# A tuned transformer block on one core: eight operand tags in the second MLP product, and the MLP norm's weights moved from the activations to w_up

## The chip, the cores and the metric

The kernel runs on one core of a Trainium2 chip. The metric is the device time of one execution in microseconds. The kernel before takes 1678.88 us (median of 3 runs, 1674.23 to 1683.34).

## The reference, cut to what matters

The block mixes tokens with two attentions, merges them, and then runs an MLP and a gated embedding on 1024 rows of width 1024, all in float32. The change lies in the MLP:

```python
x = x + merged @ w_o
h2 = rmsnorm(x, g_mlp)            # y = x * rsqrt(mean(x*x) + eps);  h2 = y * g_mlp
u = relu(h2 @ w_up)               # 1024 x 4096
x = x + (u * u) @ w_down          # 4096 x 1024
```

`g_mlp` has one weight for each of the 1024 inner columns of the first product, that is, one for each row of `w_up`.

## The kernel before, in words

Float32 operands are split into a high part (a cast) and a low part (the residue), and each block of a product is three matmuls of 128x128 by 128x512 (`mm3`). Both MLP products are done by a 2x2 block scheme with seven products in place of eight, which needs sums of blocks on both sides.

*Before the first product.* `wo` finishes x = x + merged w_o in row blocks of 128 rows: four of the upper half (h = 0), four of the lower (h = 1). `upper_rows(s)` norms an upper block, transposes it through a DMA, adds its two halves into `R0` on GpSimd (L871), multiplies by the weights on VectorE (L872, `g_up` broadcast) and makes the operands `b11` and `b21` (`parts`: a cast on ScalarE, the residue on VectorE or GpSimd). `lower_rows(s)` is a generator: its first part norms a lower block, its second transposes it on TensorE into PSUM and forms w1 = g·v(upper k) - ra, w2 = g·v(lower k) - w1 and b22 = g·v(lower k), each as four small instructions with a per-partition weight (`scaled`, L893; L902), then t3r = w2 - ra (L907) and rb = rb - w2 (L908), on GpSimd for s < 2 and on VectorE for s = 2, 3. The operands of the activations' side are b11, b21, t1 (from w1), t2 (from w2), b22, t3 (from t3r) and t4 (from rb).

*The first product.* w_up is read in column tiles of 128 (`raw_tile` or `raw2`, 128 x 8 x 128); two of them make a pair b, of 16 pairs. The order in a pair is 1 (a11, b11), 2 (a12, b21), then 6 (s2, t2), 5 (s1, t1), 3 (s4, b22), 7 (s3, t3), 4 (a22, t4), where s1 = a21 + a22, s2 = s1 - a11, s4 = a12 - s2, s3 = a11 - a21 are made on VectorE (L1038, L1039, L1043, L1047). `w_op` casts such a block on ScalarE (L815) and takes the residue on VectorE (L816), in four rotating tiles. Products 1 and 2 of the first two pairs are done early, from three tiles loaded apart (`early`), as are s1 and s2 of pair 0, on GpSimd (L955, L957). At the end of a pair the squares and their sums (`uq`, `us`) are stored to `u_d` in DRAM; `us` tiles lie in the pool `fp`.

*The second product.* For each of 4 chunks c of 1024 inner columns the products come in the order 1, 2, 5, 6, 3, 7, 4. A product has four steps k; each step takes two operands, `da` from `ua` (loaded from `u_d`) and `db` from w_down (`wd`) or from differences of its blocks (t1 to t4, `minus`, L1200, GpSimd). `operand` (L1108) numbers the operands from 0, eight to a product, gives each a tile of the pool `dp`, casts it on ScalarE (L1113) and takes the residue on VectorE (L1114). The pool `dp` is opened after `fp` is closed and takes its place in SBUF. Line 1112 picks the tile by a tag: `d0` to `d7` in turn for the first 24 operands (products 1, 2 and 5 of chunk 0), and `d0` to `d9` in turn from the 25th on.

*Order.* Engines work through their instructions in order. The order on each is set when the kernel is built, by a scheduler that goes by the program's order and by when it reckons that an instruction's inputs and its tile are there; an instruction can so come ahead of one that stands before it in the program. All DMAs of this part are issued from one queue, SyncE's, in order. With `reuse_waits="tile"` a tile of a new pool waits for just those old tiles whose memory it takes.

Of the kernel before, what the change touches and what calls it, by code (L numbers as in the profile page):

```python
# [19 lines left out]
P = 128  # L20
# [33 lines left out]
def hybrid_block_kernel(ctx: ExitStack, tc, x, p, g_mix, w_in, g_qa, w_qb, g_kva, w_kvb, g_qn, g_kn,  # L54
# [764 lines left out]
    def block_product(name, w, hop):  # L819
# [2 lines left out]
        mm3(ps, [(w[:, 0, k], w[:, 1, k], hop[:, 0, k], hop[:, 1, k]) for k in range(4)])  # L822
        return ps


    EARLY = 2
    with tc.tile_pool(name="op", bufs=2, reuse_waits="tile") as op:
        X0 = big("X0", [P, 2, 4, 512], F32)
        X1 = []

        def wo_weights(h, n):
            return quad(f"wo{h}_{n}", w_o, 256 * n, **({"pool_": op, "tag": "z"} if n % 2 else {}))

        def rows(h, s):
            return X0[:, :, s] if h == 0 else view2(X1[s])

        def wo(h, n, s, ws):
            ps = bank(f"wo{h}_{n}_{s}")
            sl = slice(s * P, (s + 1) * P)
            mm3(ps[:, :256], [(mH[h][:, k, sl], mL[h][:, k, sl]) + ws(k) for k in range(NK)])  # L840
            xs = rows(h, s)[:, n // 2, 256 * (n % 2):256 * (n % 2 + 1)]
            dve.tensor_tensor(xs, xs, ps[:, :256], ALU.add)

        def x_rows(h, s):
            r0 = (4 * h + s) * P
            nc.sync.dma_start(rows(h, s), view2(x[r0:r0 + P, :]))

        def pair(nm):
            if nm not in Hop:
                Hop[nm] = big(f"H_{nm}", [P, 2, 4, 512])  # L850
            return Hop[nm]

        def parts(nm, c0, raw, eng):

            t = pair(nm)[:, :, :, c0:c0 + P]
            act.copy(t[:, 0], raw)
            eng.tensor_tensor(t[:, 1], raw, t[:, 0].bitcast(F32), ALU.subtract)

        def upper_rows(s):

            xs, c0 = rows(0, s), s * P
            junk = op.tile([P, D], BF16, tag="junk", name=f"junk2_0_{s}", bufs=1)
            r = row_rstd(f"mlp0_{s}", xs, view2(junk), D, 2.0 ** -20)[:, 0:1]
            gb = g_up.unsqueeze(2).broadcast_to([P, NK, P])
            hl = op.tile([P, 2, D], F16, tag="nhl", name=f"nhl2_{s}", bufs=1)
            t = op.tile([P, 2, NK, P], F16, tag="nt", name=f"nt2_{s}", bufs=1)
            act.mul(view2(hl[:, 0]), xs, r)
            dve.scalar_tensor_tensor(view2(hl[:, 1]), xs, r, view2(hl[:, 0]), op0=ALU.mult, op1=ALU.subtract)
            nc.sync.dma_start(t.rearrange("p n k s -> p (n k) s"), hl.rearrange("p n k -> p (n k)"), transpose=True)
            dst = R0[:, :, c0:c0 + P]  # L870
            pool.tensor_tensor(dst, t[:, 0], t[:, 1], ALU.add)  # L871
            dve.tensor_tensor(dst, dst, gb, ALU.mult)  # L872
            parts("b11", c0, dst[:, 0:4], pool)
            parts("b21", c0, dst[:, 4:8], pool)

        def lower_rows(s):

            nc.sync.dma_start(x_d[1, :, :, s], rows(1, s))
            junk = op.tile([P, D], BF16, tag="junk", name=f"junk2_1_{s}", bufs=1)
            r = row_rstd(f"mlp1_{s}", X1[s], junk, D, 2.0 ** -20)  # L880
            yield act.mul(X1[s], X1[s], r[:, 0:1])
            c = slice(s * P, (s + 1) * P)
            ps = bank2(f"nt_mlp1_{s}")
            for k in range(NK):
                pe.transpose(ps[:, k * P:(k + 1) * P], X1[s][:, k * P:(k + 1) * P], ident)
            v = ps.rearrange("p (k s) -> p k s", k=NK)
            ra, rb = (R0[:, 4 * i:4 * i + 4, c] for i in range(2))
            t1, t2, b22 = (pair(nm)[:, :, :, c] for nm in ("t1", "t2", "b22"))
            w1, w2 = (op.tile([P, 4, P], F32, tag=f"w{i}", name=f"w{i}_{s}") for i in (1, 2))

            def scaled(o, k, t):

                return dve.scalar_tensor_tensor(o, v[:, k], g_up[:, k:k + 1], t, op0=ALU.mult, op1=ALU.subtract)  # L893

            for k in range(4):
                scaled(w1[:, k], k, ra[:, k])
            act.copy(t1[:, 0], w1)
            for k in range(4):
                scaled(w2[:, k], 4 + k, w1[:, k])
            act.copy(t2[:, 0], w2)  # L900
            for k in range(4):
                act.mul(b22[:, 0, k], v[:, 4 + k], g_up[:, 4 + k:5 + k])  # L902
            sub_f(t2[:, 1], w2, t2[:, 0])
            eng = pool if s < 2 else dve
            for k in range(4):
                scaled(b22[:, 1, k], 4 + k, b22[:, 0, k].bitcast(F32))
            eng.tensor_tensor(t3r[s], w2, ra, ALU.subtract)  # L907
            eng.tensor_tensor(rb, rb, w2, ALU.subtract)  # L908
            pool.tensor_tensor(t1[:, 1], w1, t1[:, 0].bitcast(F32), ALU.subtract)
            yield  # L910

        for s in range(4):
            x_rows(0, s)
        for n in range(4):
            ws = wo_weights(0, n)
            for s in range(4):
                wo(0, n, s, ws)
        nc.sync.dma_start(x_d[0], X0)
        R0 = big("R0", [P, NK, 512], F32)
        X1 = [op.tile([P, D], F32, tag="x1", name=f"x1_{s}", bufs=4) for s in range(4)]  # L920
        for s in range(4):
            x_rows(1, s)
        for s in range(4):
            upper_rows(s)
        for n in range(2):
            ws = wo_weights(1, n)
            for s in range(4):
                wo(1, n, s, ws)
        ws = [wo_weights(1, n) for n in (2, 3)]
        lower = [lower_rows(s) for s in range(4)]  # L930
        t3 = [op.tile([P, 2, 4, P], F32, tag=tag, name=f"t3_{tag}", bufs=1) for tag in ("nhl", "nt")]
        t3r = [t3[s // 2][:, s % 2] for s in range(4)]
        for n, s in ((2, 0), (3, 0)):
            wo(1, n, s, ws[n - 2])
        next(lower[0])
        for n, s in ((2, 1), (3, 1)):
            wo(1, n, s, ws[n - 2])
        next(lower[1])
        next(lower[0])
        for s in (2, 3):  # L940
            wo(1, 2, s, ws[0])
        early, ew = {}, []
        for n, f in enumerate((0, 2, 1)):
            t = raw_tile(f"early{f}", [P, NK, P])
            nc.sync.dma_start(t, w_up[:, f * P:(f + 1) * P].rearrange("(k p) c -> p k c", p=P))
            ew.append(t)
            for i in (1, 2) if n < 2 else ():
                early[i, n] = w_op(f"{i}_{n}", t[:, 4 * i - 4:4 * i])
        wo(1, 3, 2, ws[1])
        next(lower[2])  # L950
        next(lower[1])
        wo(1, 3, 3, ws[1])
        scaled = next(lower[3])
        s1, s2 = ew[2][:, 0:4], ew[0][:, 0:4]
        ins = pool.tensor_tensor(s1, s1, ew[2][:, 4:8], ALU.add)  # L955
        follow(ins, scaled)
        pool.tensor_tensor(s2, s1, s2, ALU.subtract)  # L957
        quarter = big("uq", [P, 2, 4, 512], F32)
        for b in range(EARLY):
            q = quarter[:, b % 2]  # L960
            act.copy(q[:, 2], block_product(f"u1_{b}", early[1, b], Hop["b11"]))
            if b < 2:
                next(lower[2 + b])
            dve.tensor_tensor(q[:, 0], block_product(f"u2_{b}", early[2, b], Hop["b21"]), q[:, 2], ALU.add)
            if b == 0:
                for i, t in ((6, s2), (5, s1)):
                    early[i, 0] = w_op(f"{i}_0", t, pool)
        for s in range(4):
            parts("t4", s * P, R0[:, 4:8, s * P:(s + 1) * P], (pool, dve)[s % 2])
        for s in range(4):  # L970
            parts("t3", s * P, t3r[s], (pool, dve)[s % 2])
# [32 lines left out]
    with tc.tile_pool(name="fp", bufs=2, reuse_waits="tile") as fp:  # L1004
# [3 lines left out]
        def up_pair(b):  # L1008
            raw = []
            for j in range(2):  # L1010
                t = (raw_tile(f"up{b}_{j}", [P, NK, P]) if b % 2 else
                     fp.tile([P, NK, P], F32, tag="raw2", name=f"raw_up{b}_{j}"))
                c0 = (2 * b + j) * P
                nc.sync.dma_start(t, w_up[:, c0:c0 + P].rearrange("(k p) c -> p k c", p=P))
                raw.append(t)
            a11, a12, a21, a22 = raw[0][:, 0:4], raw[0][:, 4:8], raw[1][:, 0:4], raw[1][:, 4:8]

            def tmp(nm):
                return fp.tile([P, 4, P], F32, tag="st", name=f"st_{nm}{b}", bufs=4)
# [19 lines left out]
            dve.tensor_tensor(s2, s1, a11, ALU.subtract)  # L1039
            u2 = plus(small("u2", f"u2_{b}"), product(6, s2, "t2"), p1)  # L1040
            p5 = product(5, s1, "t1")
            s4 = tmp("s4")
            dve.tensor_tensor(s4, a12, s2, ALU.subtract)  # L1043
            u4 = plus(small("u3", f"u4_{b}"), p5, u2)
            plus(q[:, 2], product(3, s4, "b22"), u4)
            s3 = tmp("s3")
# [60 lines left out]
    with tc.tile_pool(name="dp", bufs=1, reuse_waits="tile") as dp:  # L1107
        def operand(name, raw, eng):  # L1108
            n = nd[0]
            nd[0] += 1  # L1110

            t = dp.tile([P, 2, 512], F32R, tag=f"d{n % 8 if n < 24 else (n - 16) % 10}", name=f"d{name}")
            act.copy(t[:, 0], raw)  # L1113
            eng.tensor_tensor(t[:, 1], raw, t[:, 0].bitcast(F32), ALU.subtract)  # L1114
            return t
# [252 lines left out]
```

## Time and profile before

| | |
|---|---|
| median of 3 timed runs | 1678.88 us |
| the profiled execution's own time | 1672.75 us |
| its span | 1671.0 us |
| busy: VectorE, ScalarE, GpSimd | 73%, 49%, 44% |
| TensorE's granted clock, mean over the span | 0.974 |

The span goes from the first to the last instruction of one profiled execution. PE is TensorE, DVE VectorE, ACT ScalarE, POOL GpSimd, SP SyncE; L893 is line 893 of the kernel. "Busy" is the time in which an engine had an instruction running. A row of a timeline gives the start, the duration, the engine, the line, the operation with its output and inputs by name, the shapes and how many were merged, and in brackets the idle time before it and what ended it. The granted clock is the share of TensorE's full speed that it was allowed to run at. In the stretches below, the first MLP product lies between 871 and 1197 us, and the second between 1197 and 1534 us.

### The profile page before, as it was taken

What the parts mean: (1) busy time and instruction counts of PE and PEld (TensorE: products, weight loads), DVE (VectorE), ACT (ScalarE), POOL (GpSimd) and SP (SyncE); (2) the same over time, 40 slices, a digit from 0 to 9 for tenths busy, and PEclk for the clock granted to TensorE, in tenths of its full rate; (3) what the DMA queues carried; (4) which work ended last, traced back from release to release, by engine and by line L of the source; (5) the groups of instructions that cost most, each with busy time, mean ns of one, the idle gap of its engine ahead of it and who ended that gap; (6) DMA issues with size and microseconds to landing.
All of it is one profiled execution on the core that took longest, in us unless ns stands there. A gap on an engine that the chain in (4) does not pass through costs nothing.

```text
span 1671.0 us, 24113 instructions
## 1 busy us (share of the span) xinstructions
PE 1559.7 (93%) x8490; PEld 1320.2 (79%) x8490; DVE 1215.2 (73%) x1967; ACT 815.5 (49%) x1583; POOL 730.1 (44%) x463
## 2 busy tenths in 40 slices
PE   7999989998989888899996999999969999998898
PEld 6998877776767566688995888888758888877898
DVE  7278227776888888655467999999666878898753
ACT  6344337776988787533354222222245444435443
POOL 4254004645777777422154433333521322254653
PEclk9999999999999998999997999999979999999999
DMA  6023558999999999945544444444946353311242
GB/s 228 26 51 109 142 160 169 213 186 201 207 180 195 201 191 199 244 150 189 174 131 125 158 157 150 158 141 140 374 148 228 101 189 110 139 64 64 89 130 73
DMA packets 437865, 262.56 MB, mean 157 GB/s; under 512 B 284520, under 2 KB 383472, under 8 KB 437360
## 3 DMA queue, kind: packets, MB, share of 16 engines
q1 hardware_dynamic: 436464, 258.92, 59.2%
q10 hardware_dynamic: 1280, 2.10, 0.6%
q8 instruction: 67, 1.10, 0.3%
q14 instruction: 54, 0.44, 0.1%
HBM read 142.41 MB, written 49.35 MB: 115 GB/s over the span
## 4 chain that ended last, share of the span: by engine, by line
PE 48%; DMA 12%; DVE 10%; ACT 5%; issue 4%; POOL 4%; SPq 1%; POOLq 0%; ACTq 0%; DVEq 0%
PE u L126 17%; PE d L126 15%; DMA PT<-hl 7%; PE y L126 4%; PE wo L126 4%; PE pg L126 3%; POOL hl L602 2%; PE av L772 2%; PE gt L126 1%; ACT p L594 1%; ACT hl L600 1%; DMA wd<-in_w_down_dram 1%; DVE db L1114 1%; DVE p L591 1%; DMA bc<-rs_d 1%
## 5 line engine op out<-in xcount | busy, mean ns | idle before, releaser
L602 POOL TENSOR_TENSOR hl<-p,hl 128x1024 f16<-128x1024 f32 x128 | 279.8, 2193 | 194.8 <-PE gt L126 80.5
L126 PE MATMUL d<-db,da 128*128 128x512 f32 x1344 | 312.6, 395 | 23.3 <-ACT db L1113 16.6
L126 PEld LDWEIGHTS d<-db,da 128*128 128x128 f32 x1344 | 255.8, 191 | 79.4 <-ACT db L1113 17.0
L126 PE MATMUL u<-H_t,wop 128*128 128x512 f32 x768 | 183.6, 395 | 5.8 <-ACT H_t L900 4.6
L126 PEld LDWEIGHTS u<-H_t,wop 128*128 128x128 f32 x768 | 146.1, 191 | 38.2 <-ACT H_t L900 5.0
L591 DVE TENSOR_SCALAR_CACHE_REDUCE p<-s 128x1024 f32<-128x1024 f32 x128 | 155.6, 1218 | 16.1 <-PE s L126 5.6
L1113 ACT CAST da<-ua 128x512 fp32r<-128x512 f32 x112 | 69.6, 623 | 174.6 <-PE d L126 142.9
L594 ACT ACTIVATE p<-p,mx 128x1024 f32<-128x1024 f32 x128 | 147.2, 1150 | 9.5 <-DVE Va L458 1.5
L126 PE MATMUL u<-H_b,wop 128*128 128x512 f32 x576 | 138.2, 393 | 7.2 <-ACT wop L815 7.2
L126 PEld LDWEIGHTS u<-H_b,wop 128*128 128x128 f32 x576 | 109.4, 190 | 30.4 <-ACT wop L815 7.6
L1114 DVE TENSOR_TENSOR da<-ua,da 128x512 fp32r<-128x512 f32 x110 | 90.0, 819 | 58.2 <-ACT da L1113 58.2
L1200 POOL TENSOR_TENSOR wd<-wd,wd 128x1024 f32<-128x1024 f32 x16 | 39.8, 2492 | 195.3 <-DVE db L1114 187.4
L601 DVE TENSOR_SCALAR_CACHE_REDUCE hl<-p 128x512 f16<-128x512 f32 x128 | 87.2, 681 | 49.2 <-DMA PT<-hl 34.5
L1114 DVE TENSOR_TENSOR db<-wd,db 128x512 fp32r<-128x512 f32 x110 | 113.5, 1032 | 0.0
L126 PE MATMUL s<-KT,QT 96*128 96x512 f32 x384 | 103.5, 410 | 7.1 <-DVE p L591 6.8
L1057 POOL TENSOR_TENSOR us<-uq 128x512 f32<-128x512 f32 x15 | 19.6, 1308 | 192.9 <-DVE uq L1053 192.9
L126 PE MATMUL gt<-hH,lo_g 128*128 128x512 f32 x256 | 102.4, 400 | 1.5 <-DVE lo_g L105 1.5
L126 PE MATMUL gt<-hH,hi_g 128*128 128x512 f32 x256 | 101.9, 398 | 0.8 <-ACT hi_g L103 0.8
L126 PE MATMUL gt<-hL,hi_g 128*128 128x512 f32 x256 | 101.2, 395 | 0.0
L105 DVE TENSOR_TENSOR lo_g<-raw_g,hi_g 128x1024 fp32r<-128x1024 f32 x32 | 46.1, 1441 | 66.9 <-ACT hi_g L103 66.8
L600 ACT CAST hl<-p 128x512 f16<-128x512 f32 x128 | 78.7, 616 | 27.4 <-DMA PT<-hl 25.5
L126 PEld LDWEIGHTS s<-KT,QT 96*128 96x128 f32 x384 | 69.6, 193 | 25.2 <-DVE p L591 10.0
(341 smaller groups left out, 3930.7 us busy)
## 6 DMA issues: line engine op xcount, KB each, us to landing
ua<-u_d SPq DMA_DIRECT2D x56, 512.0 KB, 3.8
raw_g<-in_w_in_dram SPq DMA_DIRECT2D x32, 512.0 KB, 4.2
raw_up<-in_w_up_dram SPq DMA_DIRECT2D x32, 512.0 KB, 4.8
u_d<-us SPq DMA_DIRECT2D x64, 256.0 KB, 2.1
wd<-in_w_down_dram SPq DMA_DIRECT2D x16, 1024.0 KB, 9.7
u_d<-uq SPq DMA_DIRECT2D x48, 256.0 KB, 2.0
gates_d<-gst SPq DMA_DIRECT2D x32, 256.0 KB, 2.7
gg<-gates_d SPq DMA_DIRECT2D x16, 512.0 KB, 3.1
```

The lines of the kernel that those rows point to most:

```text
L105: eng.tensor_tensor(lo, raw, hi.bitcast(F32), ALU.subtract)
L126: return [pe.matmul(ps, a, b, start=start and i == 0, stop=stop and i == len(m) - 1) for i, (a, b) in list(enumerate(m))[first:last]]
L591: dve.tensor_scalar(e, ps, 1.0, 3e38, op0=ALU.mult, op1=ALU.min, accum_out=mx)
L594: act.activation(e, e, AF.Exp, bias=mx, scale=-1.0, accum_out=sums[:, hd, qt:qt + 1])
L600: act.copy(hl[:, 0, :CUT], e[:, :CUT])
L601: dve.tensor_scalar(hl[:, 0, CUT:], e[:, CUT:], 1.0, 0.0, op0=ALU.mult, op1=ALU.max, accum_out=top)
L602: pool.tensor_tensor(hl[:, 1], e, hl[:, 0], ALU.subtract)
L772: pe.matmul(av[:, :256], values(hd, kt), PT[(2 * g + half) % 3][:, n, kt], start=(kt + n == 0), stop=(kt + n == NS))
L1057: eng.tensor_tensor(v[1], q[:, 2], q[:, 3], ALU.add)
L1113: act.copy(t[:, 0], raw)
L1114: eng.tensor_tensor(t[:, 1], raw, t[:, 0].bitcast(F32), ALU.subtract)
L1200: pool.tensor_tensor(o[:, ks], a[:, ks], b[:, ks], ALU.subtract)
```

## The change

1. The multiplication by the MLP norm's weights moves from the activations to w_up: each column tile of w_up is multiplied after its load by eight instructions on ScalarE (`up_gain`), the early tiles too (35 tiles, 280 instructions). L872 goes; the small scaled instructions of the lower rows become whole ones without a weight.
2. For all four lower row blocks t3r and rb are made on GpSimd, in a third part of `lower_rows` that is called after the early products.
3. s4 of pair 0 is made early, on GpSimd, from the early tiles, and its operand too.
4. The second product's operands use the tags `d0` to `d7` throughout.

```diff
+    def up_gain(t):
+        for k in range(NK):
+            act.mul(t[:, k], t[:, k], g_up[:, k:k + 1])
...
             pool.tensor_tensor(dst, t[:, 0], t[:, 1], ALU.add)
-            dve.tensor_tensor(dst, dst, gb, ALU.mult)
...
-            for k in range(4):
-                scaled(w1[:, k], k, ra[:, k])
+            dve.tensor_tensor(w1, v[:, 0:4], ra, ALU.subtract)
             act.copy(t1[:, 0], w1)
-            for k in range(4):
-                scaled(w2[:, k], 4 + k, w1[:, k])
+            dve.tensor_tensor(w2, v[:, 4:8], w1, ALU.subtract)
             act.copy(t2[:, 0], w2)
-            for k in range(4):
-                act.mul(b22[:, 0, k], v[:, 4 + k], g_up[:, 4 + k:5 + k])
+            act.copy(b22[:, 0], v[:, 4:8])
             sub_f(t2[:, 1], w2, t2[:, 0])
-            eng = pool if s < 2 else dve
-            for k in range(4):
-                scaled(b22[:, 1, k], 4 + k, b22[:, 0, k].bitcast(F32))
-            eng.tensor_tensor(t3r[s], w2, ra, ALU.subtract)
-            eng.tensor_tensor(rb, rb, w2, ALU.subtract)
+            sub_f(b22[:, 1], v[:, 4:8], b22[:, 0])
             pool.tensor_tensor(t1[:, 1], w1, t1[:, 0].bitcast(F32), ALU.subtract)
+            yield
+            pool.tensor_tensor(t3r[s], w2, ra, ALU.subtract)
+            pool.tensor_tensor(rb, rb, w2, ALU.subtract)
             yield
...
             nc.sync.dma_start(t, w_up[:, f * P:(f + 1) * P].rearrange("(k p) c -> p k c", p=P))
+            up_gain(t)
...
                 for i, t in ((6, s2), (5, s1)):
                     early[i, 0] = w_op(f"{i}_0", t, pool)
+                pool.tensor_tensor(s4, s4, s2, ALU.subtract)
+        for s in range(4):
+            next(lower[s])
+        early[3, 0] = w_op("3_0", s4)
...
                 nc.sync.dma_start(t, w_up[:, c0:c0 + P].rearrange("(k p) c -> p k c", p=P))
+                up_gain(t)
...
-            s4 = tmp("s4")
-            dve.tensor_tensor(s4, a12, s2, ALU.subtract)
+            s4 = None
+            if b > 0:
+                s4 = tmp("s4")
+                dve.tensor_tensor(s4, a12, s2, ALU.subtract)
...
-            t = dp.tile([P, 2, 512], F32R, tag=f"d{n % 8 if n < 24 else (n - 16) % 10}", name=f"d{name}")
+            t = dp.tile([P, 2, 512], F32R, tag=f"d{n % 8}", name=f"d{name}")
```

## Rows read from the trace of the kernel before

**Rows 1.** The page's first part: busy us, share of the span, instructions.

```profile
PE 1559.7 (93%) x8490; PEld 1320.2 (79%) x8490; DVE 1215.2 (73%) x1967; ACT 815.5 (49%) x1583; POOL 730.1 (44%) x463
```

**Rows 2.** Waits of TensorE, 866 to 1560 us: total us, times, longest.

```profile
PE d L126 <- ACT db L1113: 16.6, 1, 16.6
PE u L126 <- ACT wop L815: 7.2, 1, 7.2
PE d L126 <- DVE db L1114: 6.6, 3, 2.6
```

**Rows 3.** Timeline of TensorE, 1195 to 1290 us: start, us, instruction.

```profile
1197.03 11.04 PE L126 MATMUL d<-db,da 128*128 128x512 f32 x48
1224.65 65.67 PE L126 MATMUL d<-db,da 128*128 128x512 f32 x278 [16.58 <-ACT db L1113]
```

**Rows 4.** Timeline of ScalarE, 1198 to 1240 us.

```profile
1198.60 0.61 ACT L1113 CAST db<-wd 128x512 fp32r<-128x512 f32 x1
1222.94 1.14 ACT L1113 CAST da<-ua 128x512 fp32r<-128x512 f32 x2 [23.73 <-DMA u_d<-us]
...
1237.26 0.63 ACT L1113 CAST db<-wd 128x512 fp32r<-128x512 f32 x1 [0.62 <-POOL wd L1200]
```

**Rows 5.** Chain that ended last, 1180 to 1230 us: start, us, what.

```profile
1189.19 10.16 DMA ua<-u_d
...
1218.57 4.36 DMA u_d<-us
```

**Rows 6.** Timeline of GpSimd, 1195 to 1240 us.

```profile
1203.37 4.76 POOL L1200 TENSOR_TENSOR wd<-wd,wd 128x1024 f32<-128x1024 f32 x2 [7.86 <-PE d L126]
...
1234.81 2.41 POOL L1200 TENSOR_TENSOR wd<-wd,wd 128x1024 f32<-128x1024 f32 x1 [22.09 <-DVE db L1114]
```

**Rows 7.** Stretches: busy per engine, then granted clock, DMA share, GB/s.

```profile
1208.00:1224.60 16.60, 0.07 (x1) 0.00 (x0) 1.01 (x2) 1.66 (x4) 4.72 (x3) 0.62 0.92 350
1224.60:1228.00 3.40, 3.25 (x7) 2.27 (x8) 3.29 (x6) 3.40 (x6) 0.00 (x0) 0.50 0.00 0
1228.00:1232.00 4.00, 4.00 (x17) 3.21 (x16) 2.59 (x4) 2.67 (x5) 0.00 (x0) 0.85 0.00 0
```

**Rows 8.** Timeline of SyncE's queue, 1165 to 1236 us.

```profile
1173.45 1.72 SPq L991 DMA_DIRECT2D ua<-u_d  x2
...
1194.13 0.37 SPq L991 DMA_DIRECT2D ua<-u_d  x1
```

**Rows 9.** A stretch of the last chunk: busy PE, PEld, DVE, ACT, POOL, clock.

```profile
1469.00:1491.00 22.00, 19.65 (x87) 15.95 (x85) 22.00 (x19) 9.14 (x16) 18.84 (x10) 1.00 0.16 56
```

**Rows 10.** Timeline of VectorE, 882 to 912 us.

```profile
882.73 1.13 DVE L893 SCALAR_TENSOR_TENSOR w<-nt_mlp,gc_mlp,R 128x128 f32<-128x128 f32 x4 [1.86 <-PE nt_mlp L885]
...
888.76 1.76 DVE L908 TENSOR_TENSOR R<-R,w 128x512 f32<-128x512 f32 x1
...
893.33 0.68 DVE L908 TENSOR_TENSOR R<-R,w 128x512 f32<-128x512 f32 x1
```

**Rows 11.** Timeline of TensorE, 870 to 960 us.

```profile
905.65 1.22 PE L126 MATMUL u<-H_b,wop 128*128 128x512 f32 x2 [7.16 <-ACT wop L815]
...
912.33 4.70 PE L126 MATMUL u<-H_t,wop 128*128 128x512 f32 x20
```

**Rows 12.** Timeline of ScalarE, 844 to 882 us.

```profile
871.16 1.13 ACT L902 ACTIVATE H_b<-nt_mlp,gc_mlp 128x128 fp32r<-128x128 f32 x4
```

**Rows 13.** Timeline of GpSimd, 880 to 902 us.

```profile
898.07 1.27 POOL L857 TENSOR_TENSOR H_t<-t_nhl,H_t 128x512 fp32r<-128x512 f32 x1 [5.21 <-ACT H_t L856]
```

**Rows 14.** Timeline of SyncE's queue, 880 to 912 us.

```profile
892.02 18.14 SPq L1014 DMA_DIRECT2D raw_up<-in_w_up_dram  x5
```

**Rows 15.** A pair's length in the w_up loop: busy PE, PEld, DVE, ACT, POOL.

```profile
963.00:982.00 19.00, 19.00 (x86) 15.73 (x85) 17.58 (x23) 4.85 (x8) 6.30 (x4) 1.00 0.46 152
```

**Rows 16.** Timeline of VectorE in the w_up loop, 936 to 943 us.

```profile
936.72 0.69 DVE L1038 TENSOR_TENSOR st_s<-raw_up 128x512 f32<-128x512 f32 x1 [0.42 <-DMA raw_up<-in_w_up_dram]
...
941.56 1.78 DVE L1039 TENSOR_TENSOR st_s<-st_s,raw_up 128x512 f32<-128x512 f32 x1
```

More of the change, by code (lines that the diff above doesn't have):

```diff
@@ L863, in upper_rows @@
             r = row_rstd(f"mlp0_{s}", xs, view2(junk), D, 2.0 ** -20)[:, 0:1]
-            gb = g_up.unsqueeze(2).broadcast_to([P, NK, P])
             hl = op.tile([P, 2, D], F16, tag="nhl", name=f"nhl2_{s}", bufs=1)
@@ L889, in lower_rows @@
             w1, w2 = (op.tile([P, 4, P], F32, tag=f"w{i}", name=f"w{i}_{s}") for i in (1, 2))
-            def scaled(o, k, t):
-                return dve.scalar_tensor_tensor(o, v[:, k], g_up[:, k:k + 1], t, op0=ALU.mult, op1=ALU.subtract)
-            for k in range(4):
-                scaled(w1[:, k], k, ra[:, k])
+            dve.tensor_tensor(w1, v[:, 0:4], ra, ALU.subtract)
             act.copy(t1[:, 0], w1)
-            for k in range(4):
-                scaled(w2[:, k], 4 + k, w1[:, k])
+            dve.tensor_tensor(w2, v[:, 4:8], w1, ALU.subtract)
             act.copy(t2[:, 0], w2)
-            for k in range(4):
-                act.mul(b22[:, 0, k], v[:, 4 + k], g_up[:, 4 + k:5 + k])
+            act.copy(b22[:, 0], v[:, 4:8])
             sub_f(t2[:, 1], w2, t2[:, 0])
-            eng = pool if s < 2 else dve
-            for k in range(4):
-                scaled(b22[:, 1, k], 4 + k, b22[:, 0, k].bitcast(F32))
-            eng.tensor_tensor(t3r[s], w2, ra, ALU.subtract)
-            eng.tensor_tensor(rb, rb, w2, ALU.subtract)
+            sub_f(b22[:, 1], v[:, 4:8], b22[:, 0])
             pool.tensor_tensor(t1[:, 1], w1, t1[:, 0].bitcast(F32), ALU.subtract)
+            yield
+            pool.tensor_tensor(t3r[s], w2, ra, ALU.subtract)
+            pool.tensor_tensor(rb, rb, w2, ALU.subtract)
             yield
@@ L953, in hybrid_block_kernel @@
         scaled = next(lower[3])
-        s1, s2 = ew[2][:, 0:4], ew[0][:, 0:4]
+        s1, s2, s4 = ew[2][:, 0:4], ew[0][:, 0:4], ew[0][:, 4:8]
         ins = pool.tensor_tensor(s1, s1, ew[2][:, 4:8], ALU.add)
```

## The prediction

> **What bounds the kernel now.** I read the page's first part, then TensorE's waits, then the chain of waits and the engines' timelines where those waits lie. TensorE is busy for 93% of the span [rows 1], so only a stall of TensorE that goes, or a new one, can move the time. From the end of w_o to the end of the second MLP product its waits are few: one of 16.6 us on the cast of a second-product operand, one of 7.2 us on the cast of a weight operand of the first, three that make 6.6 us on VectorE [rows 2]. The change touches the code beside each. Inside the loop over w_up no wait stands.
>
> The long wait first. Product 1 of the second MLP matmul (their order is 1, 2, 5, 6, 3, 7, 4) runs as 48 matmuls from 1197.03; the next matmul starts at 1224.65 after 16.58 us of idle time [rows 3]. On ScalarE the eighth operand cast starts at 1198.60, and then nothing until 1222.94: the engine stands before the cast of a left operand until a store of `us` to `u_d` has landed [rows 4]. The chain has that store issued at 1218.57, 4.36 us before its landing [rows 5]. A cast reads `ua` and writes an operand tile; no data comes to it from a store. What can is memory: `us` lies in the pool of the first product, and an operand tile takes its place. Which cast is it? At 1222.94 two left casts come in a row, and the right one that is then missing comes alone at 1237.26, released by GpSimd [rows 4], whose two-tile difference has just ended (1234.81 + 2.41, rows 6). That difference, t2, is read by product 6 alone, and product 6 has the operands numbered 24 to 31. Number 24 is the first for which line 1112 goes from eight tags to ten: it opens d8 in memory that this pool has not used yet. So product 6's first cast has been put ahead of product 2's, since its tile was new and waited for no matmul, and ScalarE, which works in order, holds product 2 behind a store that was late among 350 GB/s of transfers [rows 7].
>
> **The change, part by part.**
>
> *Eight tags.* Number 24 now takes d0, which is free only once product 2 has used it, so its cast can't stand ahead. What is late next? Product 2's left operand was asked for by 1175.2 [rows 8], and a load of `ua` took 10.16 us in the thick of the transfers [rows 5]. Product 5's t1 is done at 1208.13 [rows 6], while product 2 would run from 1208.07 to 1219; its later left tile is that load, landed at 1199.35. Product 6 would start at 1230, with its last left tile asked for at 1194.13 [rows 8]. So all of the 16.58 us goes. After the gap TensorE was granted 0.50 for 3.4 us and 0.85 for 4.0 us [rows 7], the level of 1.2 GHz and a mixture with 2.4: 1.7 + 0.6 = 2.3 us lost, which goes too. Gain 18.9 us.
>
> What it costs: eight tiles are four steps of two operands, ten are five. A step is 12 matmuls, 11.04 x 12 / 48 = 2.76 us [rows 3]. Products 2 and 5 had eight tags before too, and from 1224.65 TensorE ran 278 matmuls without a gap [rows 3], so there it costs nothing. In the last chunk VectorE is full, 22.00 of 22.00 us [rows 9], and TensorE runs out of operands three times [rows 2]; a lead that is one step shorter puts two more subtractions inside such a stretch, 2 x 0.68 to 2 x 1.76 us each by a VectorE instruction of that shape [rows 10]. For two stretches that is 2.7 to 7 us; below it, nothing, if the scheduler orders VectorE's work otherwise. I take 3 of 0 to 7, near the shorter row, since GpSimd isn't always running beside.
>
> *Start of the w_up loop.* The 7.16 us wait ends at 905.65 with the cast of pair 0's product 3 operand [rows 11], and VectorE is what that cast waited for: it is full from 882.73 [rows 10]. Of the work ahead of it VectorE loses: L907 and L908 for s = 2 and 3, four differences that go to GpSimd (like the two at 1.76 and 0.68 us, 4.9 us together); sixteen small scaled differences, four in 1.13 us [rows 10], that become four whole ones of 0.68 (4.5 less 2.7, 1.8 us); eight b22 residues of the same kind that become two (2.3 less 1.4, 0.9 us). That is 7.6 us. Pair 0's s4 itself goes ahead, on GpSimd, and no longer stands behind VectorE's last work before 905. ScalarE's four scaled copies per row block (1.13 us, rows 12) become one.
>
> What is late next is GpSimd, idle for 5.21 us before 898.07 [rows 13]. Now it gets s4 and four differences at some 1.27 us, 6.4 us, or 1.2 us more than that idle time; then come t3's casts and residues, so product 7 can start near 901. It also needs pair 0's raw tiles, whose loads are issued from 892.02 on [rows 14]; they come some 2 us earlier, since the store ahead of them in the queue waits for VectorE, and then get 16 multiplications; this too gives 901. Before, products 3, 7 and 4 ended at 917.03 [rows 11]; from 901 two products of 2.76 us at up to half speed end at 907 to 912. Gain 5 to 10 us; I take 7. Bounds: 11 us, where the waits of both this place and its slow matmuls go (7.2 us and some 4), and a loss of 3 us, where ScalarE, in order, stands before multiplications whose tile hasn't landed.
>
> *The gains on ScalarE.* Eight multiplications per w_up tile, 35 tiles, 280. The nearest row is the same form from PSUM, four in 1.13 us [rows 12], 0.28 us each: 79 us of ScalarE in all, 4.5 us for a pair's 16. No row shows it from SBUF; I bound it below by a quarter of a 128x512 cast and above by a whole one (0.61 us, rows 4): 2.4 to 9.8 us a pair. ScalarE is busy 4.85 of 19.00 us there [rows 15], so even the upper end fits. Cover is thin in one place: pair 3's s1 waited 0.42 us for its load at 936.72, and s2 reads s1 at 941.56 [rows 16]. Half of the 16, 2.2 us, stand between that load and s1, within the 4.1 us that are free. In the loop I cost it at nothing.
>
> The Trainium skill (ScalarE: Activation LUTs, Rules for kernel authors) speaks against this: it sends multiplications to VectorE. The row decides otherwise here: VectorE is busy 17.58 of 19.00 us [rows 15] and has no room for 4 us more.
>
> *Upper rows.* L872's four multiplications leave VectorE; TensorE had no wait there [rows 2], so nothing.
>
> **Sum.** The profiled execution took 1672.75 us (span 1671.0). 1672.75 - 18.9 - 7 + 3 = 1649.9. It was 6.1 us under the median of the timed runs, 1678.88; against that median the forecast is 1656.
>
> **Rivals.**
>
> *The stall moves.* The cast may find another late transfer, or the new order puts another one ahead. For it: the DMA engines are 0.92 busy up to 1224.6 [rows 7], and ScalarE and GpSimd get much more to reorder. Against it: product 2's own data was asked for before 1176. If the wait and its slow matmuls stay all but whole, 1656 + 18.9 = 1675. Chance 0.10.
>
> *The start gains nothing.* A VectorE difference takes 0.68 us alone and 1.76 beside GpSimd [rows 10]. Each of the five instructions that GpSimd gets can so stretch one on VectorE by 1.08 us: 5.4 of the 7.6 us come back, and GpSimd's own chain becomes the late one. 1656 + 7 = 1663; with the loss of 3, 1666. Chance 0.15. The Trainium skill (SBUF — State Buffer, Who interferes with whom) has it as a rule: a VectorE instruction with two SBUF inputs contends with GpSimd's reads. These rows agree.
>
> *Slower: the multiplications bind VectorE.* Place: s1 in the w_up loop. If VectorE's queue stands for all 4.5 us before s1 with nothing ready behind it, a pair needs 17.58 + 4.5 = 22.1 us of VectorE, where TensorE's 84 matmuls of a pair take about 19 (86 touch a stretch of 19.00 us, rows 15): 3 us in each of 14 pairs, 42 us, so 1698. It decides from 1.4 us of wait per pair on. For it: s1 follows its load closely [rows 16]. Against it: half of the 16 belong to the tile that is loaded first, and s2 leaves room. Chance 0.08.
>
> **Numbers.** Forecast 0.67, its own range 1645 to 1667 (start +11 to 0, tags 0 to 7, some 3 from run to run). About 0.5%, 8.4 us, is what a measurement of this kernel can tell from no change. Faster, under 1670.5: the forecast and the start's rival, 0.82, rounded to 0.81. Same: the moved stall and its like, 0.11. Slower 0.08. Range 1644 to 1674.
>
> **What would show it.** Right: the 16.6 us wait before the 49th matmul `d` is gone, product 2's casts follow at a step's pitch, and the granted clock stays at 1.00 there; the idle time ahead of the first product 3 of w_up is mostly gone; ScalarE has some 79 us more of busy time, and TensorE no wait between 920 and 1190. Wrong: a wait of TensorE in the w_up loop, one above 5 us in the first chunk of the second product, or over 14 us of waits in its last.

## The result and the profile after

The changed kernel takes 1721.08 us (median of 4 runs), the kernel before 1680.54 us beside it: ratio 1.0239, 95% interval 1.0208 to 1.027, so 2.4% slower. The forecast was 1656 us with a range of 1644 to 1674. It was wrong in sign and size. The two profiled executions differ by 47.5 us (1672.75 and 1720.25 us), more than the medians' 40.5, since the one before ran below its median.

Where the time went is read from four marks in the two profiled executions: TensorE's first matmul of the first MLP product (`u`), its first of the second (`d`), its last `d`, and the end of the span.

| us | before | after | difference |
|---|---|---|---|
| up to the first product | 871.0 | 875.3 | +4.3 |
| first product | 326.1 | 381.0 | **+54.9** |
| second product | 336.6 | 324.8 | -11.8 |
| behind it | 137.3 | 137.3 | 0 |

The 4.3 us in front are not explained. In the profiled executions of this study that mark lies between 871 and 882 us; it lies at 878.0 in a kernel without any multiplication by the weights (e7), and it differs by 2.1 us between two kernels that are the same up to the second product (before and e1).

In the first product TensorE's waits make 50.1 us after and 12.9 us before. That is 37 of the 54.9 us; the other 18 are matmuls that took longer (330.9 us of busy time after, 313.1 before), of which the last section shows some.

The waits of TensorE from 860 to 1560 us after (total us, times, longest), against [rows 2]:

```profile
PE u L126 <- ACT wop L815: 30.3, 12, 7.2
PE u L126 <- ACT H_t L897: 8.9, 1, 8.9
PE d L126 <- DVE db L1116: 6.7, 7, 3.6
PE u L126 <- DVE wop L816: 6.4, 8, 1.0
PE u L126 <- DVE u L1027: 4.4, 3, 2.1
```

The wait of 16.6 us on `db` is gone, as forecast; in its place the weight operands (`wop`) of the first product make TensorE wait again and again. The page's groups of instructions after name the new ones (busy us, mean ns, then the idle time of the engine before them and its cause):

```profile
L828 ACT ACTIVATE raw_up<-raw_up,gc_mlp 128x128 f32<-128x128 f32 x256 | 77.2, 388 | 105.0 <-DMA raw_up<-in_w_up_dram 82.0
```

The 256 multiplications of the loop take 77 us, 0.30 us each, close to the prediction's 0.28 (its 79 us are for 280). But ScalarE stands 105 us before them, 82 of it for loads of w_up. The other 23 us are three waits in which a sum on VectorE ended 0.02 to 0.06 us behind the load and so has the name. What stands behind the multiplications in ScalarE's queue? One pair of the loop, first ScalarE, after:

```profile
1050.14 0.62 ACT L815 CAST wop<-raw_up 128x512 fp32r<-128x512 f32 x1 [2.10 <-PE u L126]
1058.03 4.79 ACT L828 ACTIVATE raw_up<-raw_up,gc_mlp 128x128 f32<-128x128 f32 x16 [7.27 <-DMA raw_up<-in_w_up_dram]
1062.73 0.60 ACT L815 CAST wop<-raw_up 128x512 fp32r<-128x512 f32 x1
```

The first cast is product 1's operand, the last one product 2's. Between them stand sixteen multiplications that neither needs: eight of the pair's own second tile and eight of the *next* pair's first tile. Then the queue that loads the tiles:

```profile
1053.04 1.55 SPq L1014 DMA_DIRECT2D raw_up<-in_w_up_dram  x2
...
1076.64 1.55 SPq L1014 DMA_DIRECT2D raw_up<-in_w_up_dram  x2
```

and VectorE beside it:

```profile
1052.29 0.68 DVE L1050 TENSOR_TENSOR st_s<-raw_up,raw_up 128x512 f32<-128x512 f32 x1
...
1056.62 0.68 DVE L1027 TENSOR_TENSOR u<-u,u 128x512 f32<-128x512 f32 x1
1063.36 0.69 DVE L816 TENSOR_TENSOR wop<-raw_up,wop 128x512 fp32r<-128x512 f32 x1 [6.06 <-ACT wop L815]
...
1075.89 0.68 DVE L1050 TENSOR_TENSOR st_s<-raw_up,raw_up 128x512 f32<-128x512 f32 x1
```

Read the three together. L1050 is s3 = a11 - a21 of the pair before, the last reader of an old tile. It ends at 1052.97, and the load into that tile's memory is issued at 1053.04; the load of the second tile comes right behind it (it waits for product 4's residue, VectorE's next but one). ScalarE starts to multiply at 1058.03 and casts at 1062.73. VectorE, which has had no work ahead of that cast's residue since 1057.3, goes on at 1063.36. From the end of s3 to the residue are 10.4 us. From there VectorE works through its queue for 13.2 us to the end of the next s3, at 1076.57, and the next load goes out at 1076.64. That is a cycle through four queues. This turn of it takes 23.6 us, about what a pair takes (730 matmuls in 200 us are 23.0 us a pair on the mean, by 84 matmuls a pair; before it was 19). So the engines as a whole, over 200 us of the loop (busy PE, PEld, DVE, ACT, POOL with counts, granted clock, DMA share, GB/s), after, beside [rows 15]:

```profile
950.00:1150.00 200.00, 178.60 (x730) 140.23 (x729) 153.68 (x195) 75.52 (x196) 54.55 (x35) 0.96 0.39 128
```

VectorE's wait for the late cast in the same 200 us, after:

```profile
DVE wop L816 <- ACT wop L815: 45.7, 8, 6.5
```

153.7 us busy and 45.7 us before that one cast: 199.4 of 200. TensorE (178.6) isn't the bound there any more. The second product, TensorE after, against [rows 3]:

```profile
1256.33 5.83 PE L126 MATMUL d<-db,da 128*128 128x512 f32 x25
1262.98 13.94 PE L126 MATMUL d<-db,da 128*128 128x512 f32 x60 [0.82 <-DVE db L1116]
```

### The profile page after: what moved, and what is told of

It is laid out like the page before. It is cut to its first block, busy times and chain, and to the rows that moved or that the text cites. A ratio compares the mean times of both kernels' runs of the same rounds, so it can differ in the third digit from the quotient of the medians.

```text
span 1718.5 us, 24328 instructions
## 1 busy us (share of the span) xinstructions
PE 1579.2 (92%) x8490; PEld 1322.9 (77%) x8490; DVE 1216.0 (71%) x1922; ACT 891.8 (52%) x1851; POOL 744.2 (43%) x468
## 5 line engine op out<-in xcount | busy, mean ns | idle before, releaser
L126 PE MATMUL d<-db,da 128*128 128x512 f32 x1344 | 311.7, 393 | 10.3 <-DVE db L1116 10.1
L126 PE MATMUL u<-H_b,wop 128*128 128x512 f32 x576 | 156.0, 418 | 33.6 <-ACT wop L815 23.1
L594 ACT ACTIVATE p<-p,mx 128x1024 f32<-128x1024 f32 x128 | 147.3, 1150 | 9.3 <-DVE Va L458 1.5
L828 ACT ACTIVATE raw_up<-raw_up,gc_mlp 128x128 f32<-128x128 f32 x256 | 77.2, 388 | 105.0 <-DMA raw_up<-in_w_up_dram 82.0
L1116 DVE TENSOR_TENSOR da<-ua,da 128x512 fp32r<-128x512 f32 x110 | 105.5, 959 | 29.4 <-ACT da L1115 29.3
L1202 POOL TENSOR_TENSOR wd<-wd,wd 128x1024 f32<-128x1024 f32 x16 | 45.8, 2863 | 176.2 <-DVE db L1116 167.7
```

Of the source, the lines that this page charges most:

```text
L126: return [pe.matmul(ps, a, b, start=start and i == 0, stop=stop and i == len(m) - 1) for i, (a, b) in list(enumerate(m))[first:last]]
L594: act.activation(e, e, AF.Exp, bias=mx, scale=-1.0, accum_out=sums[:, hd, qt:qt + 1])
L828: act.mul(t[:, k], t[:, k], g_up[:, k:k + 1])
L1202: pool.tensor_tensor(o[:, ks], a[:, ks], b[:, ks], ALU.subtract)
```

## The experiments

A table first; the ratio is to the kernel before in the same series, with its 95% interval, the stages are of the profiled execution.

| kernel | us | ratio | first product | second product |
|---|---|---|---|---|
| e1 eight tags alone | 1662.5 | 0.9925 (0.9902 to 0.9948) | 326.0 | 323.4 |
| e2 no multiplication in the loop | 1661.0 | 0.992 (0.9895 to 0.9946) | 325.6 | 321.9 |
| e3 multiplications behind later casts | 1665.1 | 0.9947 (0.9921 to 0.9972) | 327.5 | 324.9 |
| e4 multiplications on GpSimd | 1688.1 | 1.0065 (1.0046 to 1.0084) | 349.2 | 324.9 |
| e5 one multiplication a tile | 1704.1 | 1.0161 (1.0129 to 1.0194) | 362.0 | 326.1 |
| e6 e3 with twice as many | 1674.1 | 0.9978 (0.9962 to 0.9994) | 332.7 | 324.7 |
| e7 no multiplication at all | 1662.3 | 0.9915 (0.9888 to 0.9942) | 323.7 | 322.0 |
| e8 e1, pair 0's differences early | 1687.9 | 1.0058 (1.0035 to 1.008) | 323.6 | 344.8 |
| e9 no squares | 1693.8 | 1.0091 (1.0063 to 1.0119) | 354.4 | 322.7 |
| e10 e8 with `st` at its old place | 1662.2 | 0.9901 (0.988 to 0.9922) | 325.5 | 325.0 |
| e11 tiles of three pairs | 1673.0 | 0.9981 (0.9965 to 0.9997) | 329.3 | 327.4 |

### e1: eight tags alone

```diff
-            t = dp.tile([P, 2, 512], F32R, tag=f"d{n % 8 if n < 24 else (n - 16) % 10}", name=f"d{name}")
+            t = dp.tile([P, 2, 512], F32R, tag=f"d{n % 8}", name=f"d{name}")
```

> The kernel before with one part of the change alone: the second product's operands use eight tags throughout. Theory (the operand of product 6 that opened new memory is what held ScalarE): the 16.6 us stall and its 2.3 us of slow clock go, and the last chunk gives some of it back, so 12 to 19 us less than the kernel before, 1662 to 1669 us. Rival (the stall finds another late transfer): within 3 us of the kernel before. In the changed kernel the second product was 11.8 us shorter, so less than 8 us here would mean that another part of the change also helped there.

Measured 13.6 us under the kernel before, with a second product shorter by 13.2 us. TensorE there, e1:

```profile
1199.12 13.99 PE L126 MATMUL d<-db,da 128*128 128x512 f32 x61
1214.14 3.06 PE L126 MATMUL d<-db,da 128*128 128x512 f32 x12 [1.02 <-DVE db L1114]
1217.54 72.83 PE L126 MATMUL d<-db,da 128*128 128x512 f32 x319 [0.35 <-DVE db L1114]
```

The 16.58 us of [rows 3] have become 1.4 us. This part of the change works by itself, and by about as much as it does inside the change (13.2 and 11.8 us).

### e2: no multiplication in the loop

```diff
                 nc.sync.dma_start(t, w_up[:, c0:c0 + P].rearrange("(k p) c -> p k c", p=P))
-                up_gain(t)
                 raw.append(t)
```

> The changed kernel without the multiplications of the w_up tiles that are loaded inside the loop (it leaves the MLP norm's weights out of them; the three early tiles keep theirs). Theory (the 54.9 us that the first product lost are due to these multiplications alone): the first product goes back to 326 us or a few us less, so 1660 to 1668 us. Rival (the other parts, GpSimd's new differences and s4, cost the loop something too): above 1680 us.

The first product takes 325.6 us. All of the 54.9 us hang on these 256 multiplications, and none on the differences that went to GpSimd or on s4.

### e3: the same multiplications, later in ScalarE's queue

```diff
+                if j == 0: up_gain(t, casts[f"5_{b - 2}"] if b > 1 else None)
...
+            up_gain(raw[1], casts[f"3_{b - 1}"] if b > 0 else None)
```

`casts` holds the casts by product and pair; each multiplication is ordered behind the one that is named.

> The changed kernel with the same multiplications on ScalarE, but ordered behind casts that come some 6 us after their load is asked for: a pair's first tile behind the cast of product 5 two pairs earlier, its second tile behind the cast of product 3 one pair earlier. Theory (ScalarE in order stands before multiplications whose tile is still on its way, some 7 us a pair, and the four operand tiles of lead cover 8 us less the 5 us of the multiplications themselves): no wait of ScalarE on a w_up load above 1 us, first product about 326 to 330 us, in all 1664 to 1672 us. Rival (it is the 4.8 us of multiplications a pair, or a later s1 on VectorE): most of the 54.9 us stays, above 1700 us.

As the theory said: 327.5 us. ScalarE in e3:

```profile
1039.88 0.62 ACT L815 CAST wop<-st_s 128x512 fp32r<-128x512 f32 x1 [2.05 <-DVE uq L1056]
1040.41 2.45 ACT L828 ACTIVATE raw_up<-raw_up,gc_mlp 128x128 f32<-128x128 f32 x8
...
1043.75 2.45 ACT L828 ACTIVATE raw_up<-raw_up,gc_mlp 128x128 f32<-128x128 f32 x8
1046.10 0.61 ACT L815 CAST wop<-st_s 128x512 fp32r<-128x512 f32 x1
```

The sixteen stand where their tiles have landed before, with no idle time ahead of them, and TensorE is busy for 200.00 of 200 us. The work is unchanged, only its place is. So the cost isn't ScalarE's time.

### e4: the multiplications on GpSimd

```diff
-                up_gain(t)
+                pool.tensor_tensor(t, t, g_up.unsqueeze(2).broadcast_to([P, NK, P]), ALU.mult)
```

> The changed kernel with the multiplications of the loop's tiles on GpSimd, one instruction of 128x1024 a tile. Theory: ScalarE no longer stands before a load; GpSimd does instead, but it has only the sums of the squares behind it, which nobody waits for soon: first product 326 to 335 us, in all 1664 to 1677 us. Rival (VectorE's differences take 1.76 us instead of 0.68 us beside GpSimd; a tile is some 2.3 us by the 1.2 us of a 128x512 difference, 4.6 us a pair, so VectorE's 17.6 us a pair become up to 22 against TensorE's 19): up to 3 us in each of 14 pairs, 1700 to 1712 us.

349.2 us, between the two. A tile takes 1.97 us, and what it holds up is VectorE's s1. VectorE in e4:

```profile
1046.32 0.69 DVE L1050 TENSOR_TENSOR st_s<-raw_up,raw_up 128x512 f32<-128x512 f32 x1
...
1052.32 0.69 DVE L1027 TENSOR_TENSOR uq<-u,u 128x512 f32<-128x512 f32 x1
1056.05 0.69 DVE L1039 TENSOR_TENSOR st_s<-raw_up 128x512 f32<-128x512 f32 x1 [3.04 <-POOL raw_up L1015]
```

and GpSimd in e4:

```profile
1052.07 3.95 POOL L1015 TENSOR_TENSOR raw_up<-raw_up,gc_mlp 128x1024 f32<-128x1024 f32 x2 [8.74 <-DMA raw_up<-in_w_up_dram]
```

Ten such waits make 20.1 us in 200, and VectorE is busy for the other 179.6. This is the prediction's third rival at its own place, on another engine: 2.0 us a pair before s1, more than the 1.4 us that VectorE had free. The theory was wrong in that somebody does wait for GpSimd soon. Of the rival's reason there is a little: VectorE's own work is 18.2 us a pair (179.6 us in which TensorE ran 827 matmuls) where it was 17.6 before [rows 15]. The cycle is here as well, with GpSimd in ScalarE's place: 9.0 us from the end of s3 (1047.01) to s1, 11.4 us on to the end of the next s3 (1067.48), 20.5 together, against 20.3 us a pair on the mean.

### e5: one multiplication a tile, at the changed kernel's place

```diff
-                up_gain(t)
+                up_gain(t, 1)
```

> The changed kernel with one multiplication for each tile in the loop in place of eight, at the same place in ScalarE's queue (seven eighths of the weights are left out there). The wait for the load stays, the 4.8 us of multiplications a pair shrink to some 0.7 us. Theory (wait and multiplications together must fit into the lead of the casts, three products or 8.2 us): 7.3 us of wait + 0.7 us just fit, so the first product takes 326 to 340 us and the kernel 1660 to 1677 us. Rival (any wait for a load ahead of the casts costs its own length): most of the 54.9 us stays, above 1700 us.

A miss: 362.0 us, two thirds of the loss with an eighth of the work. ScalarE in e5:

```profile
1045.68 0.62 ACT L815 CAST wop<-raw_up 128x512 fp32r<-128x512 f32 x1 [2.10 <-PE u L126]
1054.38 0.40 ACT L828 ACTIVATE raw_up<-raw_up,gc_mlp 128x128 f32<-128x128 f32 x1 [8.08 <-DMA raw_up<-in_w_up_dram]
1056.07 0.40 ACT L828 ACTIVATE raw_up<-raw_up,gc_mlp 128x128 f32<-128x128 f32 x1 [1.28 <-DMA raw_up<-in_w_up_dram]
1056.38 0.60 ACT L815 CAST wop<-raw_up 128x512 fp32r<-128x512 f32 x1
```

and VectorE in e5:

```profile
1048.95 0.68 DVE L1050 TENSOR_TENSOR st_s<-raw_up,raw_up 128x512 f32<-128x512 f32 x1
...
1057.02 0.69 DVE L816 TENSOR_TENSOR wop<-raw_up,wop 128x512 fp32r<-128x512 f32 x1 [4.39 <-ACT wop L815]
```

ScalarE waits 9.4 us, not 7.3: the loads come when they are released, and the work that fell away in front of them is waited out. So "wait plus work against the lead of the casts" was not the right sum, and the cycle was looked for instead: here 7.4 us from s3 to the residue and 14.4 us on to the next s3, 21.8, against a pair of 21.9 us (768 matmuls in 200 us).

### e6: e3 with each multiplication done twice

Against e3:

```diff
             (follow if after else lambda a, b: a)(act.mul(t[:, k], t[:, k], g_up[:, k:k + 1]), after)
+            [act.mul(t[:, k], t[:, k], v) for v in again]
```

> The kernel e3 (multiplications behind the casts) with each of the loop's multiplications followed by a second one, by 1.0: 9.6 us of multiplications a pair, so ScalarE is busy some 14.5 of 19 us. Theory (it is the place in the queue, not the work): within 8 us of e3, 1660 to 1674 us. Rival (ScalarE's work itself, 4.8 us a pair, costs time): up to 4.8 us in each of 14 pairs more than e3, 1700 to 1732 us.

1674.1 us, 0.1 over the theory's upper end and far under the rival. ScalarE is busy 131 of 200 us, TensorE 200 of 200. The 5.2 us more of the first product are one wait at its start (11.6 us where e3 has 5.8).

### e7: no multiplication at all

```diff
             t = raw_tile(f"early{f}", [P, NK, P])
...
-            up_gain(t)
...
-                up_gain(t)
```

> The changed kernel without any multiplication by the weights, neither in the loop nor of the three early tiles (it leaves the MLP norm's weights out). It differs from the kernel of the second run by 24 multiplications on ScalarE ahead of the loop, 7.3 us. Theory (these stand before the lower rows' chain on ScalarE and eat what VectorE gains at the start): TensorE's wait for t1 and t2 falls from 6.2 us to 4.6 us or less, and the whole is 2 to 7 us shorter than that kernel, 1654 to 1659 us. Rival (the start gains nothing since the differences on GpSimd are the late ones): no shorter, 1659 to 1663 us.

In the whole it is no shorter than e2 (1662.3 to 1661.0 us, ratios 0.9915 and 0.992); the first product alone is 1.9 us shorter. TensorE's waits in e7:

```profile
PE u L126 <- ACT wop L815: 7.5, 1, 7.5
...
PE u L126 <- ACT H_t L897: 2.5, 1, 2.5
...
PE u L126 <- DVE H_t L808: 2.4, 1, 2.4
```

The wait for t2 falls from 6.2 us in e2 to 2.5, but the next long one, for product 7's operand, grows from 5.3 to 7.5. The rival held, and for the reason that it gave: the last difference on GpSimd (L904) holds a cast on ScalarE, that cast holds VectorE, and s3 and its cast come behind. In e7:

```profile
902.02 0.62 ACT L861 CAST H_t<-R 128x512 fp32r<-128x512 f32 x1 [3.54 <-POOL R L904]
902.67 1.11 DVE L862 TENSOR_TENSOR H_t<-R,H_t 128x512 fp32r<-128x512 f32 x1 [4.30 <-ACT H_t L861]
```

What the start gains in one place it waits for in the next.

### e8: pair 0's differences all early

```diff
+        follow(pool.tensor_tensor(s4, s4, s2, ALU.subtract), low[3])
+        early[3, 0] = w_op("3_0", s4, pool)
+        early[7, 0] = w_op("7_0", s3, pool, low[3])
```

Made from e1; `low[3]` is GpSimd's last residue of t1, and s3 of pair 0 is made early too, beside s1 and s2.

> The kernel of the first run (eight tags alone) with all four differences of pair 0 made early from the early tiles on GpSimd, the operands of products 3 and 7 too, behind GpSimd's last residue of t1; pair 0 then needs no s1 to s4 on VectorE and one load less. Weights and t3r, rb stay as in the kernel before. Theory (the 7.1 us wait there is the cast of product 3's operand, which stands behind VectorE's whole queue): that wait goes, and the next late thing is t3, some 3 us behind the end of product 5, so 4 to 8 us less, 1654 to 1659 us. Rival (GpSimd's five new instructions push t4 and t3 back): no gain, 1661 to 1664 us.

25 us *slower* than e1 (22 by the two ratios, each to the kernel before beside it). The first product gained 2.5 us; the second lost 21.4. TensorE in e8:

```profile
1198.93 8.32 PE L126 MATMUL d<-db,da 128*128 128x512 f32 x36
1227.18 8.39 PE L126 MATMUL d<-db,da 128*128 128x512 f32 x25 [19.93 <-ACT db L1127]
```

ScalarE in e8:

```profile
1224.51 0.62 ACT L1127 CAST da<-ua 128x512 fp32r<-128x512 f32 x1 [23.40 <-DMA u_d<-us]
1226.51 0.62 ACT L1127 CAST db<-wd 128x512 fp32r<-128x512 f32 x1 [1.38 <-DMA u_d<-us]
```

The stall is back, with eight tags and in the fourth step of product 1 (36 matmuls are three steps). Pair 0 no longer opened `st`, so that tag came to lie behind `us` in the pool, and d6 and d7 over `us`.

### e9: the changed kernel without the squares

```diff
-            for i in (0, 2, 3, 1):
+            for i in ():
                 dve.scalar_tensor_tensor(q[:, i], q[:, i], 0.0, q[:, i], op0=ALU.max, op1=ALU.mult)
```

ScalarE's order is held as it is in the changed kernel, by the means of e3.

> The changed kernel, with ScalarE's order as it is there, without the four squares a pair on VectorE in the w_up loop (it leaves max(x, 0) * x out, so sums and stores read the bare product). Between 950 and 1150 us of the changed kernel VectorE is busy 153.7 us and stands 45.7 us before the residue that waits for the late cast: 199.4 of 200. Theory now (VectorE is the bound: its work and its idle time in order add up to the pair; TensorE's waits follow from that): the squares are 32.7 of 200 us there, 3.9 us of a pair of 23.5 us, so a pair falls to some 19.5 to 20.5 us and the first product from 381 to 320 to 335 us; in all 1665 to 1680 us. Rival (the casts' lead of four operand tiles is what is too short against ScalarE's 12 us away): a pair stays at 23 us or more, 1712 to 1721 us.

354.4 us: outside both. The squares are off VectorE, and half of the loss goes, but not all. The cycle says why: the squares shorten only the stretch that lies behind the residue, 11.3 us instead of 13.2; the stretch with the load, 10.1 us, stays, and VectorE waits longer in it. VectorE in e9, and its wait from 950 to 1150 us:

```profile
1042.60 0.69 DVE L1050 TENSOR_TENSOR st_s<-raw_up,raw_up 128x512 f32<-128x512 f32 x1
...
1053.37 0.69 DVE L816 TENSOR_TENSOR wop<-raw_up,wop 128x512 fp32r<-128x512 f32 x1 [6.47 <-ACT wop L815]
```

```profile
DVE wop L816 <- ACT wop L815: 54.8, 9, 6.8
```

Together that is 21.4 us there, against a pair of 21.05 us on the mean (798 matmuls in 200 us). "VectorE's work and a fixed idle time" was too simple: the idle time is what the load leaves over.

### e10: e8 with `st` at its old place

```diff
+            if b == 0:
+                pool.tensor_tensor(tmp("s1"), a21, a22, ALU.add)
+            else:
```

> The kernel e8_early_pair with one more sum on GpSimd in pair 0 that nobody reads, whose only effect is that the tile `st` gets its place in the pool fp ahead of u2, u3 and us, as in the kernel before. By the sizes that are written in the kernel (raw2 2 x 4 KB, p1 4 x 2, st 4 x 2, u2 and u3 2 x 2 each, us 5 x 2; an operand tile 4 KB) operand tile d6 lies over u2 with st in its old place and over us with st behind us, as in e8. Theory (that tile's cast waits for the store of us): the 19.9 us stall goes with its slow matmuls, some 21 us, 1656 to 1663 us. Rival (the stall is due to later loads or another order at the start): 1680 us or more stays.

The stall is gone (second product 325.0 us), by one sum that nobody reads. So it is memory that holds such a cast, and the layout of the pool before decides which. The gain at the start is not clear of noise: 1662.2 us here, 1662.5 in e1, and 4 us less by the two ratios, whose intervals overlap. e10's waits of TensorE:

```profile
PE u L126 <- ACT H_t L904: 7.3, 1, 7.3
PE u L126 <- DVE wop L816: 1.7, 1, 1.7
...
PE u L126 <- POOL H_t L913: 1.5, 1, 1.5
PE u L126 <- ACT wop L815: 1.2, 1, 1.2
```

The wait of 7.1 us for `wop` that e1 has is gone, but the wait for t2 is 2.6 us longer (4.7 in e1), and there are 1.5 us before t1 and 2.9 before two operands.

### e11: room for the tiles of three pairs

```diff
-                t = (raw_tile(f"up{b}_{j}", [P, NK, P]) if b % 2 else
-                     fp.tile([P, NK, P], F32, tag="raw2", name=f"raw_up{b}_{j}"))
+                t = (raw_tile(f"up{b}_{j}", [P, NK, P]) if b % 3 == 1 else
+                     fp.tile([P, NK, P], F32, tag="raw2", name=f"raw_up{b}_{j}", bufs=4))
```

> The changed kernel with room for the w_up tiles of three pairs in place of two (raw2 four tiles, for two of every three pairs; us four and p1 three tiles to make room), and ScalarE's order held as it is there: both tiles' 16 multiplications between the casts of products 1 and 2. Theory now (a cycle through the queues: VectorE's s3 releases a tile, SyncE loads it, ScalarE multiplies, then casts product 2's operand, VectorE takes the residue and works on to the next s3; 10.4 us from s3 to the residue and 13.2 us from there to the next s3 are the 23.6 us of a pair): with a load released a pair earlier nothing in the cycle waits for it, 4.8 us of multiplications fit before the cast, no wait of ScalarE on a load above 1 us, the first product 326 to 333 us, in all 1662 to 1673 us. Rival (multiplications ahead of that cast cost time wherever their tile's load stands): the first product above 345 us, 1683 us or more.

329.3 us. ScalarE in e11:

```profile
1051.34 0.62 ACT L815 CAST wop<-raw_up 128x512 fp32r<-128x512 f32 x1 [2.10 <-PE u L126]
1051.87 4.79 ACT L828 ACTIVATE raw_up<-raw_up,gc_mlp 128x128 f32<-128x128 f32 x16
1056.57 0.60 ACT L815 CAST wop<-raw_up 128x512 fp32r<-128x512 f32 x1
```

The queue is the changed kernel's: cast, sixteen multiplications, cast. The load was released a pair earlier, so nothing waits: TensorE is busy for 200.00 of 200 us again. What cost the 54.9 us is the release of the tile together with that place; neither the multiplications nor their place cost more than 3.2 us of the first product by themselves (327.5 and 329.3 us against 326.1 before). In all the kernel takes 1673.0 us, at the upper edge of what was expected: 16.9 us of waits at the start and 11.6 in the second product remain.

## Why the prediction was wrong, point by point

*Eight tags, -18.9 us and +3.* Right in mechanism. e1 gives -13.6 us (8.7 to 16.4 us by the ratio's interval) where the two terms make -15.9. They can be told apart by the time from the first matmul `d` to the 1151st (it stands ahead of the last chunk's waits in both), which is 279.9 us before and 262.9 in e1: -17.0 us, where the sum has -18.9 (1.4 us of small waits stay in e1's first chunk); from there to the last one it is 56.3 and 60.2 us: the lost lead costs 3.9 us in the last chunk, where the sum has 3 (the other kernels with eight tags have 58.6 to 61.5 us there). That operand 24 lay over `us` was inferred; e8 and e10 show the thing itself, a cast of another operand number held by a store of `us` as soon as the layout puts it there. The cure is so less sure than the prediction has it: eight tags help while d0 to d7 lie over other tags.

*Start of the w_up loop, -7 us.* Wrong; it is nothing that can be measured in the whole. With the relief and no multiplication in the way (e7) the kernel takes 1662.3 us, without the relief (e1) 1662.5; the first product alone is 2.3 us shorter. The prediction had product 7 start near 901 us, 30 us behind the first matmul `u`; in e7 it starts at 914.04, 36 us behind it. The rival "the start gains nothing" (0.15) held, with its reason as the rows of e7 show it: GpSimd's chain becomes the late one. The lower end, a loss of 3 us, was seen in one wait: in the changed kernel the cast of t2 stands behind five multiplications on a tile of the loop, and TensorE waits 8.9 us for it (6.2 in e2).

*The gains on ScalarE, "in the loop I cost it at nothing".* **This is the step that failed**: nothing was forecast, 54.9 us were measured. The argument was ScalarE's busy time, 4.85 of 19.00 us [rows 15], and the size of a multiplication, which came out as forecast (0.30 us each, 16 in 4.79). Both are right and neither is what counts. A multiplication takes part in the order of its queue; it waits for a load, and what stands behind it waits too. The prediction asked this question for VectorE's s1 [rows 16], and for ScalarE only at the start of the loop (its loss of 3 us), not for the casts inside it, though it had read in [rows 4] what one waiting instruction there does. The second question that wasn't asked is who lets the load start: s3 on VectorE, and VectorE stood behind the casts. That closes the cycle of 23.6 us, and the pair goes from 19 to 23 us.

*The third rival (0.08, 1698 us).* The nearest of all: VectorE bound by an in-order wait, from 1.4 us a pair on, since only that much of its pair is free [rows 15]. Place and price differed: not s1 but product 2's residue (L816), not 4.5 us but 5.3 us a pair on the mean (45.7 us over 8.7 pairs). At s1 it is seen in e4.

*What would show it wrong* was "a wait of TensorE in the w_up loop", and that is what the trace shows.

The row on VectorE's room (17.58 of 19.00) decided in the prediction against the rule that the Trainium skill has (ScalarE: Activation LUTs, Rules for kernel authors), that multiplications belong on VectorE. e3 and e11 show that ScalarE can take them at little cost: 327.5 and 329.3 us of first product against 326.1, and no wait of TensorE between 950 and 1150 us. That VectorE could not have taken them was not run. What neither the row nor the rule says is where in a queue they go.

Not settled: the 4.3 us ahead of the first product, and what would shorten the start of the loop; in e7 GpSimd sets it, and each relief tried there moved the wait. That the layout of a pool can be read off the written sizes was tried at one place (e8 against e10).

No version beats e1 by more than can be measured: it is 0.75% faster than the kernel before with one changed line, and e10 (1662.2 us, 0.99% faster, intervals that overlap) is not clearly ahead of it.

## What to carry to other kernels

Before work is put on an engine with free time, write down what will stand behind it in that engine's queue, what it waits for, and who releases that; if the releaser itself waits for what stands behind, the sum of that ring becomes the pitch of the loop when it is longer than the old one. The cheap cures are the place (order the work behind instructions that come after its data has landed) and one more buffer, so that the release lies a turn earlier; less work at the same place helps little (with an eighth of it, two thirds of the loss stayed). And a stall on a store before a cast that reads nothing of it is a matter of memory: see which old tile the new one lies over.

## What the runs showed of the hardware that was not expected

A gap of TensorE costs more than its length, but not always. TensorE behind one gap of the changed kernel, and then the clock (busy PE, granted clock, DMA share, GB/s) of four stretches; the second follows that gap of 2.40 us, the fourth one of 1.74 us:

```profile
1063.38 4.86 PE L126 MATMUL u<-H_b,wop 128*128 128x512 f32 x12 [2.40 <-ACT wop L815]
```

```profile
1058.10:1060.90 2.80, 2.80 (x13) 1.00 0.25 63
1063.40:1068.20 4.80, 4.80 (x13) 0.64 0.17 64
1068.20:1073.50 5.30, 5.30 (x25) 1.00 0.39 148
1086.30:1089.50 3.20, 3.18 (x13) 1.00 0.02 5
```

After the first, the 12 matmuls of a product took 4.86 us instead of 2.88, between the levels of 1.2 and 2.4 GHz, so 2 us on top of 2.4; after the other the clock stayed, and they took 3.29 us. In e9 a gap of 1.78 us was followed by 0.64 as well, in e5 gaps of 1.76 and 1.78 us by 1.00: the length of the gap alone doesn't tell.

A multiplication of 128x128 by a weight for each partition on ScalarE takes 388 ns by itself and 0.30 us in a row of sixteen. The Trainium skill (ScalarE: Activation LUTs, What ACT_TABLE_LOAD costs) has 186 ns and 0.833 ns a column, 93 ns more for an operand that is a pointer, and 93 ns of overlap back to back. An estimate from these figures is 386 and 293 ns, and the traces agree. The same work on GpSimd is 1.97 us for a tile of 128x1024 (e4), against 2.45 us for the eight on ScalarE (e3).
